# Two directions of a chunked scan: issued one after the other, or in step with each direction in its half of the array

## The chip, the cores and the metric

One core of one Trainium2 chip runs the whole program. The metric is the device time of one execution in microseconds (us); the time of a kernel is the median over its runs. Engines are named as in the profile: PE (TensorE matmul), PEld (TensorE weight load), DVE (VectorE), ACT (ScalarE), POOL (GpSimd), SP (SyncE, which issues the transfers).

## The reference, cut to what matters

The program is a hybrid attention block (two layers) followed by a second block: a gated delta-rule scan over 256 context rows, then the same scan over the 256 latent rows, starting from the state that the context left; then an output projection and a mixture of 16 experts. The scan runs in two directions, forwards and on the flipped sequence, and the two outputs are added. Each direction has 4 heads of width 128 and goes through 4 chunks of 64 rows:

```python
def step(state, xs):
    q_i, k_i, u_i, w_i, a_i, gl_i = xs
    v_new = u_i - w_i @ state
    o_i = q_i @ state + a_i @ v_new
    state = state * jnp.exp(gl_i)[..., None, None] + jnp.swapaxes(k_i, -1, -2) @ v_new
    return state, o_i
...
o_f, s_f = gdn_chunked(q, k, v, g[:, :, 0], beta[:, :, 0], s0_f)
o_b, s_b = gdn_chunked(flip(q), flip(k), flip(v), flip(g[:, :, 1]), flip(beta[:, :, 1]), s0_b)
return o_f + flip(o_b), s_f, s_b
```

The context scan needs only its final states; the latent scan needs the outputs, and not its last state.

## The kernel before, in words

The 256 rows lie in two tiles of 128 partitions (`tt`); each tile holds two chunks of 64 rows, one in partitions 0 to 63 and one in 64 to 127 (`HALF`). Direction `d` = 0 goes through the chunks 0, 1, 2, 3 and `d` = 1 through 3, 2, 1, 0. So at step `st` the one direction is always in one half of the partitions and the other direction in the other half.

`gdn_uw` (L1388) makes, for each of the four pairs (`tt`, `d`), `u` and `w` of both chunks of the tile. It transposes `v` (L1264), scales it with beta into `vb` (DVE, L1396) and `k` into `kb` (POOL, L1398), multiplies `G` with `vb` in `chunk_dots` (L1316; the two halves of the partitions in turn, all into one PSUM bank), copies the result to `U[tt, d]` (ACT, L1401), multiplies `kb` with `G` (L1406, the two halves in turn into two banks) and copies that to `WT[tt, d]` (ACT, L1409).

`gdn_scan` (L1424) is a generator. For each step it does direction 0 and then direction 1, and yields after each: `W` times state (L1444: all 128 rows of the array, 64 of its columns, 4 products), the sum into 64 partitions of `U` (DVE, L1445), the decay of the state (POOL, L1448), for the latent rows `Q` times state into the output bank (L1451: again 128 rows and 64 columns), `kg` times `U` (L1457: 64 rows and 128 columns) and the new state (ACT L1460 in the first context step, else DVE L1462). `kg` itself is made once for each pair (POOL, L1440; two buffers). After every second step the latent scan adds `aT` times `U` for both halves (L1467). An fp32 product stands in the trace as two matmul records, so 4 products are x8.

Around it: `block2` zips the context scan with `tinv_64` of the latent rows (a chain of 16 links of a `chunk_dots` and a DVE sum, L1537 to L1547), and the latent scan with `parts`, which are `chunk_mlp` (projections at L433 to L435 and L457, a gelu, norms and a product at L1595) and `scan_gate` (two more projections). The source only sets priorities: a list planner of the tile framework orders each engine's queue when the program is built, which is why projections that stand later in the source (L433 to L435 for `v` and `q`) lie in PE's queue between the products of the scan.

PSUM: `bank()` hands out five banks; the latent scan holds two of them for its outputs. SBUF: the pools of block 2 lie one behind the other in the order of `B2`, where `kg` stands in the middle. The expert weights are fetched ahead of time into a ring of 21 buffers (`ring`, 1 MB each) that lie over the same memory, and into the 2 buffers `w` of the projections; each fetch waits on SP's queue until what lay there is used up. The fetches of the projections (`load2`, L1179) and of the output projection (`rows_out`, L466) go through the same queue.

Of the kernel before, what the change touches and what calls it, by code (L numbers as in the profile page):

```python
# [32 lines left out]
HALF = slice(0, 64), slice(64, 128)  # L33
XB = 4
# [213 lines left out]
class Kern:  # L248
# [1125 lines left out]
    def gdn_attn(self, R):  # L1374
# [3 lines left out]
        for tt in range(2):  # L1378
# [5 lines left out]
            for d in range(2):  # L1384
                R["aT", tt, d] = aT[:, 8 * d + 4 * tt:8 * d + 4 * tt + 4, :]
                self.nc.vector.tensor_mul(R["aT", tt, d], self.decay(R, tt, d), kq)

    def gdn_uw(self, R):  # L1388

        nc = self.nc  # L1390
        G = R["G"]
        for tt in range(2):
            pv = self.nat(R, "v", tt)
            for d in range(2):
                vb = self.blk("vb", 2)
                nc.vector.tensor_mul(vb, pv, self.per_row(R["beta"][:, tt, 4 * d:4 * d + 4]))  # L1396
                kb = self.blk("kb", 2)
                nc.gpsimd.tensor_mul(kb, R["hat", "k", tt], self.per_row(R["be"][:, tt, d, :]))  # L1398
                pu = self.chunk_dots(G[tt, d], vb)
                R["U", tt, d] = self.blk("Ub" if tt ^ d else "Ua", 2)  # L1400
                nc.scalar.copy(R["U", tt, d], pu)  # L1401

                pw = [self.bank()[:, :, :64] for _ in HALF]
                for h in range(4):
                    for b, p in zip(HALF, pw):
                        nc.tensor.matmul(p[:, h, :], kb[b, h, :], G[tt, d][b, h, :], start=True, stop=True)  # L1406
                R["WT", tt, d] = self.blk("Wb" if tt ^ d else "Wa", 2)
                for b, p in zip(HALF, pw):
                    nc.scalar.copy(R["WT", tt, d][:, :, b], p)  # L1409

# [13 lines left out]
    def gdn_scan(self, R, S=None):  # L1424


        nc = self.nc
        o = None
        if S is not None:
            R["o"] = o = [self.bank() for _ in range(2)]  # L1430
        kg, touched = {}, set()
        S = S or [None, None]
        for st in range(4):
            for d in range(2):
                tt, hf = divmod(st if d == 0 else 3 - st, 2)
                rows = slice(64 * hf, 64 * hf + 64)
                U = R["U", tt, d]
                if (tt, d) not in kg and not (o and st == 3):
                    kg[tt, d] = self.blk("kg", 2)
                    nc.gpsimd.tensor_mul(kg[tt, d], R["hat", "k", tt], self.per_row(R["eg"][:, 1, tt, d, :]))  # L1440
                if S[d] is not None:
                    p = self.bank()
                    for h in range(4):
                        nc.tensor.matmul(p[rows, h, :], R["WT", tt, d][:, h, rows], S[d][:, h, :], start=True, stop=True)  # L1444
                    nc.vector.tensor_add(U[rows], U[rows], p[rows])  # L1445
                    if not (o and st == 3):
                        Se = self.blk("X", XB)
                        nc.gpsimd.tensor_mul(Se, S[d], self.per_row(R["egl"][:, 2 * tt + hf, 4 * d:4 * d + 4]))  # L1448
                if o:
                    for h in range(4):  # L1450
                        nc.tensor.matmul(o[tt][rows, h, :], R["Q", tt, d][:, h, rows], S[d][:, h, :],  # L1451
                                         start=(h == 0 and (tt, hf) not in touched), stop=False, skip_group_check=True)
                    touched.add((tt, hf))
                if not (o and st == 3):
                    p = self.bank()
                    for h in range(4):
                        nc.tensor.matmul(p[:, h, :], kg[tt, d][rows, h, :], U[rows, h, :], start=True, stop=True)  # L1457
                    n = self.blk("S", 4)
                    if S[d] is None:
                        nc.scalar.copy(n, p)  # L1460
                    else:
                        nc.vector.tensor_add(n, Se, p)  # L1462
                    S[d] = n
                if o and st % 2:
                    for h in range(4):
                        for b in HALF:
                            nc.tensor.matmul(o[tt][b, h, :], R["aT", tt, d][b, h, :], U[b, h, :], start=False, stop=False,  # L1467
                                             skip_group_check=True)
                yield
        R["S"] = S  # L1470

    def tinv_16(self, A, C, O, L, M, T):
# [474 lines left out]
```

## Time and profile before

| | |
|---|---|
| time, median of 3 runs | 1303.93 us (1303.8 to 1306.29) |
| the profiled execution's own time | 1295.95 us |
| its span in the profile | 1294.2 us |
| busy, share of the span | PE 81%, PEld 57%, DVE 43%, ACT 30%, POOL 20% |
| mean granted TensorE clock | 0.893 |
| HBM read and written | 328.6 MB, 254 GB/s over the span |

The rows below come from the one profiled execution. Its own time is the span plus the 1.75 us that lie around it; it is 8 us under the median of the runs, so a sum made from the rows is a difference, which is then taken off the median.

### The profile page before, as it was taken

Reading aid. Unit: us, or ns where it says so; the run is one execution under the profiler, and the core shown is the slowest. Engines: PE = TensorE matmul, PEld = TensorE weight load, DVE = VectorE, ACT = ScalarE, POOL = GpSimd, SP = SyncE. Lnnn points to the kernel's source line nnn. Section 1 sums busy time; section 2 is a strip of 40 time slices with the busy share of each in tenths; the row PEclk is TensorE's granted clock in tenths of the full one; section 3 lists DMA queues with packets and bytes.
Section 4 is the critical chain, followed back from the end, with each engine's and each line's share of the span. In section 5 each row is a group of like instructions: output and inputs, shape, how many; then the busy total and the mean of one; then the engine's idle time right before and its main releaser. Section 6 shows DMA issues by size and latency. Waiting matters only on the chain.

```text
span 1294.2 us, 22853 instructions
## 1 busy us (share of the span) xinstructions
PE 1048.7 (81%) x9488; PEld 733.4 (57%) x9488; DVE 558.6 (43%) x1315; ACT 387.4 (30%) x899; POOL 264.6 (20%) x235
## 2 busy tenths in 40 slices
PE   5878999986869999957879999898666766676665
PEld 2766787776757876736778888654322432232232
DVE  2585357777696445586585435620100010010002
ACT  2334337635334425525542434310000000000002
POOL 1431132266421221152424343200000000000000
PEclk9899999999989999977979999899877787787777
DMA  8745864434224385521211555979999999999996
GB/s 357 263 160 204 311 228 171 140 130 176 102 88 168 140 305 191 215 78 39 95 58 40 192 202 215 363 288 417 421 420 419 421 419 420 419 420 420 420 421 247
DMA packets 52569, 330.07 MB, mean 255 GB/s; under 512 B 8049, under 2 KB 9969, under 8 KB 14321
## 3 DMA queue, kind: packets, MB, share of 16 engines
q1 hardware_dynamic: 52464, 328.61, 64.9%
q8 instruction: 74, 1.21, 0.4%
q14 instruction: 31, 0.25, 0.1%
HBM read 327.54 MB, written 1.05 MB: 254 GB/s over the span
## 4 chain that ended last, share of the span: by engine, by line
PE 42%; DMA 35%; DVE 11%; POOL 4%; ACT 4%; issue 4%; POOLq 0%; SPq 0%; DVEq 0%; ACTq 0%
DMA rw<-in_w_up 13%; DMA rw<-in_w_down 11%; DMA rw<-in_w_gate 5%; PE mm L433 4%; PE mm L435 4%; PE mm L434 4%; DMA w<-in_w_up 3%; PE s L476 3%; PE mm L457 3%; PE g L372 3%; DMA wg<-in_w_ada 3%; POOL wl L345 2%; PE s L1316 2%; ACT wh L344 2%; PE s L553 2%
## 5 line engine op out<-in xcount | busy, mean ns | idle before, releaser
L433 PE MATMUL mm<-uT,wh 128*128 128x256 f32 x576 | 173.1, 301 | 11.1 <-DVE yT L1247 6.6
L435 PE MATMUL mm<-uT,wl 128*128 128x256 f32 x576 | 167.7, 294 | 15.9 <-DVE wl L345 9.2
L344 ACT CAST wh<-w 128x1024 fp32r<-128x1024 f32 x124 | 127.6, 1033 | 154.1 <-PE mm L434 114.9
L434 PE MATMUL mm<-uT,wh 128*128 128x256 f32 x576 | 167.4, 291 | 0.0
L345 POOL TENSOR_TENSOR wl<-w,wh 128x1024 fp32r<-128x1024 f32 x47 | 114.2, 2431 | 200.3 <-ACT wh L344 168.1
L435 PEld LDWEIGHTS mm<-uT,wl 128*128 128x128 f32 x576 | 111.6, 195 | 25.9 <-DVE wl L345 10.1
L433 PEld LDWEIGHTS mm<-uT,wh 128*128 128x128 f32 x576 | 112.6, 196 | 22.7 <-issue 14.5
L1808 PE MATMUL g<-rw,XE 128*32 128x256 f32 x928 | 84.2, 469 | 41.3 <-DMA rw<-in_w_up 41.3
L345 DVE TENSOR_TENSOR wl<-w,wh 128x1024 fp32r<-128x1024 f32 x77 | 96.6, 1254 | 43.9 <-ACT wh L344 43.5
L434 PEld LDWEIGHTS mm<-uT,wh 128*128 128x128 f32 x576 | 112.4, 195 | 5.2 <-issue 4.0
L1808 PE MATMUL o<-rw,XE 128*32 128x256 f32 x944 | 85.3, 464 | 32.8 <-DMA rw<-in_w_gate 32.8
L1824 DVE TENSOR_TENSOR hd<-hd,g 128x256 f32<-128x256 f32 x16 | 6.7, 419 | 214.4 <-PE g L1808 214.4
L1820 ACT ACTIVATE hd<-o 128x256 f32<-128x256 f32 x16 | 6.1, 384 | 310.9 <-PE o L1808 310.9
L1852 PE MATMUL mm<-rw,hT 128*32 128x256 f32 x880 | 67.9, 446 | 18.7 <-DMA rw<-in_w_down 13.2
L1808 PEld LDWEIGHTS g<-rw,XE 128*32 128x32 f32 x928 | 31.8, 128 | 86.1 <-DMA rw<-in_w_up 66.8
L1808 PEld LDWEIGHTS o<-rw,XE 128*32 128x32 f32 x944 | 31.1, 125 | 76.8 <-DMA rw<-in_w_gate 53.9
L457 PE MATMUL mm<-wh,uT 128*128 128x256 f32 x256 | 54.0, 298 | 3.1 <-ACT wh L344 2.5
L1852 PEld LDWEIGHTS mm<-rw,hT 128*32 128x32 f32 x880 | 27.9, 124 | 49.5 <-DMA rw<-in_w_down 21.7
L457 PEld LDWEIGHTS mm<-wh,uT 128*128 128x128 f32 x256 | 41.6, 194 | 7.1 <-ACT wh L344 2.9
L565 ACT ACTIVATE P<-s,nm 128x256 f32<-128x256 f32 (+1 forms) x88 | 35.8, 419 | 18.9 <-DVE nm L558 18.7
L476 PE MATMUL s<-wh,m 128*128 128x512 f32 x128 | 41.2, 401 | 0.0
L457 PE MATMUL mm<-wl,uT 128*128 128x256 f32 x128 | 37.9, 296 | 0.8 <-DVE wl L345 0.7
(644 smaller groups left out, 1987.9 us busy)
## 6 DMA issues: line engine op xcount, KB each, us to landing
rw<-in_w_gate SPq DMA_DIRECT2D x59, 1024.0 KB, 19.9
rw<-in_w_up SPq DMA_DIRECT2D x58, 1024.0 KB, 19.9
rw<-in_w_down SPq DMA_DIRECT2D x55, 1024.0 KB, 19.8
w<-in_w_in SPq DMA_DIRECT2D x48, 1024.0 KB, 4.7
wg<-in_w_mod SPq DMA_DIRECT2D x24, 1024.0 KB, 4.9
wg<-in_w_ada SPq DMA_DIRECT2D x21, 1024.0 KB, 5.3
w<-in_w_out SPq DMA_DIRECT2D x12, 1024.0 KB, 4.8
w<-in_w_up SPq DMA_DIRECT2D x6, 1024.0 KB, 19.8
```

Source lines behind the costliest of these rows:

```text
L344: self.nc.scalar.copy(hi, w)
L345: self.lo_engine().tensor_sub(lo, w, hi)
L372: nc.tensor.matmul(p[32 * j:32 * j + 32, :], vec[:, 2 * q + kk, :], w[:, kk, 256 * j:256 * j + 256], start=(kk == 0 and (q == 0 or not who ...
L433: mm(out, wh[:, k, :], uh[:, k, :], start=(k == 0), stop=False)
L434: mm(out, wh[:, k, :], ul[:, k, :], start=False, stop=False)
L435: mm(out, wl[:, k, :], uh[:, k, :], start=False, stop=(k == 7))
L457: mm(p[:, tt, :], a[:, k, t], b[:, k % 4, :], start=(k == 0 and tt == 0 and j == 0), stop=(k == 7 and j == 2), skip_group_check=True)
L476: mm(Y(tt, n), a[:, t], b[:, 512 * n:512 * n + 512], start=(k2 == 0 and kk == 0 and i == 0), stop=(k2 == 3 and kk == 1 and i == 2))
L553: nc.tensor.matmul(S[:, h, o:o + n], qT[rows, t], kT[rows, :n], start=False, stop=True, skip_group_check=True)
L565: nc.scalar.activation(Pm[:, h, o:o + n], S[:, h, o:o + n], AF.Exp, bias=nm[:, i:i + 1], scale=0.125, accum_out=l[:, i:i + 1])
L1808: nc.tensor.matmul(pp[32 * j:32 * j + 32, :], XE[:, k, 32 * (e % 4):32 * (e % 4) + 32], w[:, kk, 256 * j:256 * j + 256], start=(k == 0), s ...
L1852: nc.tensor.matmul(py[32 * j:32 * j + 32, :], hT[:, cb, 32 * jj:32 * jj + 32], w[:, kk, 256 * j:256 * j + 256], start=(k == 0), stop=(k == 7))
```

## The change

`gdn_scan` does a step for both directions at once. For each head it issues the product of direction 0 and then that of direction 1, whose operands or results lie in the other half of the partitions; `W` times state of both directions goes into one bank, and one DVE sum of 128 partitions takes it into `U`. `kg` times `U` goes into two banks. `Q` times state now comes after `kg` times `U`, and `aT` times `U` follows in every step. The scan yields twice after each step. For this `U` is laid out by steps: `U[st]` holds the chunk of direction 0 in its half and that of direction 1 in the other. `gdn_uw` therefore transposes both tiles of `v` at the start, goes through the pairs as (0, 0), (1, 1) and then (1, 0), (0, 1), and for each two makes two `u` products and then two `w` products. `kg` gets four buffers in place of two.

```diff
--- before.py
+++ after.py
@@ -1385,26 +1385,39 @@
                 R["aT", tt, d] = aT[:, 8 * d + 4 * tt:8 * d + 4 * tt + 4, :]
                 self.nc.vector.tensor_mul(R["aT", tt, d], self.decay(R, tt, d), kq)
 
+    @staticmethod
+    def step_of(st):
+
+
+        return [(c // 2, HALF[c % 2]) for c in (st, 3 - st)]
+
     def gdn_uw(self, R):
 
         nc = self.nc
         G = R["G"]
-        for tt in range(2):
-            pv = self.nat(R, "v", tt)
-            for d in range(2):
-                vb = self.blk("vb", 2)
-                nc.vector.tensor_mul(vb, pv, self.per_row(R["beta"][:, tt, 4 * d:4 * d + 4]))
-                kb = self.blk("kb", 2)
-                nc.gpsimd.tensor_mul(kb, R["hat", "k", tt], self.per_row(R["be"][:, tt, d, :]))
-                pu = self.chunk_dots(G[tt, d], vb)
-                R["U", tt, d] = self.blk("Ub" if tt ^ d else "Ua", 2)
-                nc.scalar.copy(R["U", tt, d], pu)
+        pv = [self.nat(R, "v", tt) for tt in range(2)]
+        for s2 in range(0, 4, 2):
+            vb, kb = {}, {}
+            pairs = [(s2 // 2, 0), (1 - s2 // 2, 1)]
+            for tt, d in pairs:
+                vb[tt, d] = self.blk("vb", 2)
+                nc.vector.tensor_mul(vb[tt, d], pv[tt], self.per_row(R["beta"][:, tt, 4 * d:4 * d + 4]))
+                kb[tt, d] = self.blk("kb", 2)
+                nc.gpsimd.tensor_mul(kb[tt, d], R["hat", "k", tt], self.per_row(R["be"][:, tt, d, :]))
+            for st in (s2, s2 + 1):
+                pu = self.bank()
+                for h in range(4):
+                    for d, (tt, b) in enumerate(self.step_of(st)):
+                        nc.tensor.matmul(pu[b, h, :], G[tt, d][b, h, :], vb[tt, d][b, h, :], start=True, stop=True)
+                R["U", st] = self.blk("Ub" if s2 else "Ua", 2)
+                nc.scalar.copy(R["U", st], pu)
+            for tt, d in pairs:
 
                 pw = [self.bank()[:, :, :64] for _ in HALF]
                 for h in range(4):
                     for b, p in zip(HALF, pw):
-                        nc.tensor.matmul(p[:, h, :], kb[b, h, :], G[tt, d][b, h, :], start=True, stop=True)
-                R["WT", tt, d] = self.blk("Wb" if tt ^ d else "Wa", 2)
+                        nc.tensor.matmul(p[:, h, :], kb[tt, d][b, h, :], G[tt, d][b, h, :], start=True, stop=True)
+                R["WT", tt, d] = self.blk("Wb" if s2 else "Wa", 2)
                 for b, p in zip(HALF, pw):
                     nc.scalar.copy(R["WT", tt, d][:, :, b], p)
 
@@ -1431,42 +1444,50 @@
         kg, touched = {}, set()
         S = S or [None, None]
         for st in range(4):
-            for d in range(2):
-                tt, hf = divmod(st if d == 0 else 3 - st, 2)
-                rows = slice(64 * hf, 64 * hf + 64)
-                U = R["U", tt, d]
-                if (tt, d) not in kg and not (o and st == 3):
-                    kg[tt, d] = self.blk("kg", 2)
+            at = list(enumerate(self.step_of(st)))
+            more = not (o and st == 3)
+            U = R["U", st]
+            for d, (tt, b) in at:
+                if (tt, d) not in kg and more:
+                    kg[tt, d] = self.blk("kg", 4)
                     nc.gpsimd.tensor_mul(kg[tt, d], R["hat", "k", tt], self.per_row(R["eg"][:, 1, tt, d, :]))
-                if S[d] is not None:
-                    p = self.bank()
-                    for h in range(4):
-                        nc.tensor.matmul(p[rows, h, :], R["WT", tt, d][:, h, rows], S[d][:, h, :], start=True, stop=True)
-                    nc.vector.tensor_add(U[rows], U[rows], p[rows])
-                    if not (o and st == 3):
-                        Se = self.blk("X", XB)
-                        nc.gpsimd.tensor_mul(Se, S[d], self.per_row(R["egl"][:, 2 * tt + hf, 4 * d:4 * d + 4]))
-                if o:
-                    for h in range(4):
-                        nc.tensor.matmul(o[tt][rows, h, :], R["Q", tt, d][:, h, rows], S[d][:, h, :],
-                                         start=(h == 0 and (tt, hf) not in touched), stop=False, skip_group_check=True)
-                    touched.add((tt, hf))
-                if not (o and st == 3):
-                    p = self.bank()
-                    for h in range(4):
-                        nc.tensor.matmul(p[:, h, :], kg[tt, d][rows, h, :], U[rows, h, :], start=True, stop=True)
-                    n = self.blk("S", 4)
+            Se = [None, None]
+            if S[0] is not None:
+                p = self.bank()
+                for h in range(4):
+                    for d, (tt, b) in at:
+                        nc.tensor.matmul(p[b, h, :], R["WT", tt, d][:, h, b], S[d][:, h, :], start=True, stop=True)
+                nc.vector.tensor_add(U, U, p)
+                if more:
+                    for d, (tt, b) in at:
+                        Se[d] = self.blk("X", XB)
+                        e = 2 * tt + (b.start > 0)
+                        nc.gpsimd.tensor_mul(Se[d], S[d], self.per_row(R["egl"][:, e, 4 * d:4 * d + 4]))
+            if more:
+                p = [self.bank() for _ in range(2)]
+                for h in range(4):
+                    for d, (tt, b) in at:
+                        nc.tensor.matmul(p[d][:, h, :], kg[tt, d][b, h, :], U[b, h, :], start=True, stop=True)
+                N = [self.blk("S", 4) for _ in range(2)]
+                for d in range(2):
                     if S[d] is None:
-                        nc.scalar.copy(n, p)
+                        nc.scalar.copy(N[d], p[d])
                     else:
-                        nc.vector.tensor_add(n, Se, p)
-                    S[d] = n
-                if o and st % 2:
-                    for h in range(4):
-                        for b in HALF:
-                            nc.tensor.matmul(o[tt][b, h, :], R["aT", tt, d][b, h, :], U[b, h, :], start=False, stop=False,
-                                             skip_group_check=True)
-                yield
+                        nc.vector.tensor_add(N[d], Se[d], p[d])
+            if o:
+                for h in range(4):
+                    for d, (tt, b) in at:
+                        nc.tensor.matmul(o[tt][b, h, :], R["Q", tt, d][:, h, b], S[d][:, h, :],
+                                         start=(h == 0 and (tt, b.start) not in touched), stop=False, skip_group_check=True)
+                touched.update((tt, b.start) for d, (tt, b) in at)
+                for h in range(4):
+                    for d, (tt, b) in at:
+                        nc.tensor.matmul(o[tt][b, h, :], R["aT", tt, d][b, h, :], U[b, h, :], start=False, stop=False,
+                                         skip_group_check=True)
+            if more:
+                S = N
+            yield
+            yield
         R["S"] = S
 
     def tinv_16(self, A, C, O, L, M, T):
```

## Rows read from the trace of the kernel before

**Rows 1.** Windows: stretch, length, busy us by engine (instructions), granted clock, DMA share, GB/s.

```profile
676.00:727.00 51.00, 49.74 (x609) 43.56 (x608) 25.29 (x46) 17.55 (x31) 19.78 (x17) 0.98 0.22 74
727.00:748.00 21.00, 17.40 (x153) 14.68 (x151) 10.48 (x16) 10.04 (x30) 8.15 (x8) 0.92 0.69 250
748.00:802.00 54.00, 53.10 (x441) 47.98 (x442) 25.20 (x37) 21.14 (x33) 20.78 (x19) 1.00 0.51 181
802.00:830.00 28.00, 25.47 (x121) 19.48 (x120) 18.99 (x31) 13.17 (x34) 7.74 (x4) 1.00 0.89 348
830.00:852.00 22.00, 17.97 (x106) 14.42 (x109) 10.55 (x41) 3.49 (x10) 0.00 (x0) 0.77 0.63 263
```

**Rows 2.** PE's waits from 676 to 802: us in total, times, longest.

```profile
PE s L1457 <- DVE Ub L1445: 1.3, 1, 1.3
```

**Rows 3.** Critical chain, 796 to 880: start, us until the next piece, what.

```profile
855.76 12.88 DMA rw<-in_w_up
```

**Rows 4.** Windows of 640 to 830 for L1444, for L1457 and for L1451 alone: PE, PEld.

```profile
640.00:830.00 190.00, 15.22 (x112) 11.85 (x112) 0.95 0.45 163
...
640.00:830.00 190.00, 16.93 (x112) 13.98 (x112) 0.95 0.45 163
...
640.00:830.00 190.00, 8.72 (x64) 7.15 (x64) 0.95 0.45 163
```

**Rows 5.** Critical chain, 640 to 830: start, us until the next piece, what.

```profile
684.91 1.02 PE s L1444 x8
...
687.07 1.08 PE s L1457 x8
...
749.92 0.87 PE s L1451 x8
```

**Rows 6.** Timeline, PE, 714 to 728: start, length, line, form; halves of the partitions in turn.

```profile
717.47 1.09 PE L1316 MATMUL s<-vb,E 64*64 64x128 f32 x16
718.49 1.11 PE L1406 MATMUL s<-E,kb 64*128 64x64 f32 x16
719.53 0.66 PE L1264 MATMUL s<-c,yT 128*128 128x128 f32 x4
```

**Rows 7.** Timeline, PE, 107.4 to 112: products in column strips, in row halves, in the whole array.

```profile
107.52 1.07 PE L372 MATMUL g<-wg,cv 128*32 128x256 f32 x16
...
108.83 0.92 PE L553 MATMUL s<-qk 64*128 64x256 f32 x8
109.69 1.13 PE L400 MATMUL g<-gacc,c 128*128 128x256 f32 x4
```

**Rows 8.** Timeline, one step of one direction in the context scan.

```profile
684.84 1.09 PE L1444 MATMUL s<-S,Wa 128*64 128x128 f32 x8
...
685.96 0.68 DVE L1445 TENSOR_TENSOR Ua<-Ua,s 64x512 f32<-64x512 f32 x1 [0.54 <-PE s L1444]
...
687.00 1.16 PE L1457 MATMUL s<-Ua,kg 64*128 64x128 f32 x8
...
688.26 0.69 DVE L1462 TENSOR_TENSOR S<-X,s 128x512 f32<-128x512 f32 x1 [1.62 <-PE s L1457]
```

**Rows 9.** Instructions of L1448 and of L1401: count, shortest, median and longest in ns.

```profile
L1448 POOL TENSOR_TENSOR X<-S,legl x6: 1040/1041/1245, 708.0 to 774.7; 128x512 f32<-128x512 f32 x6
...
L1401 ACT COPY Ua<-s x4: 586/586/586, 649.8 to 724.3; 128x512 f32<-128x512 f32 x4
```

**Rows 10.** Waits of SP's queue over the span: us in total, times, longest.

```profile
SPq L1846 <- PE s L1457: 14.2, 1, 14.2
```

**Rows 11.** Timeline, SP, 700 to 900: issues of the output projection's weights.

```profile
790.62 0.33 SPq L466 DMA_DIRECT2D w<-in_w_out  x1
...
799.78 0.33 SPq L466 DMA_DIRECT2D w<-in_w_out  x1
```

**Rows 12.** The page, transfers: count, KB each, median us from issue to landing.

```profile
rw<-in_w_gate SPq DMA_DIRECT2D x59, 1024.0 KB, 19.9
...
w<-in_w_out SPq DMA_DIRECT2D x12, 1024.0 KB, 4.8
```

## The prediction, made before the result was known

> **What bounds the kernel now.** I read the windows by stage first. From 676 to 727 (the context scan beside a chain of the latent inverse) PE is busy 49.74 of 51 us, and from 748 to 802 (the latent scan beside the projections) 53.10 of 54; apart from its own weight loads no other engine is over half busy in either [rows 1]. In between, from 727 to 748, PE has only 17.40 of 21 us: there a chain through ACT, DVE and POOL sets the pace. The waits say the same: the longest that PE has in the scans on a sum of theirs is 1.3 us [rows 2]. So both scans are bound by the work in PE's queue, not by the latency of a step: the planner has put projections into the holes. A faster step therefore gains only as far as PE time is removed, and then it gains nearly all of that.
>
> What comes after decides whether the gain lasts. In 830 to 852 the transfers rest (DMA share 0.63) [rows 1]: the weight buffers are full before the first expert product frees one. Then PE waits 12.88 us for a weight in one piece [rows 3], and the rest is bound by transfers. Their second run begins when the first buffer comes free, so time taken off before 852 should move the whole tail forward, as long as the prefetch is still complete. From 727 to 852 the DMA engines rest 21 × 0.31 + 54 × 0.49 + 28 × 0.11 + 22 × 0.37 = 44 us [rows 1], more than the change can take away.
>
> **The change part by part.** *Products of the scan.* L1444 has 112 records, L1457 112, L1451 64 [rows 4], that is 14, 14 and 8 groups of 8 records. A group holds PE for 1.02, 1.08 and 0.87 us until the next piece [rows 5]: 14.3 + 15.1 + 7.0 = 36.4 us. In the changed kernel the same records stand in 7, 7 and 4 groups of 16, in which neighbours lie in different halves of the array.
>
> What does a group of 16 cost? The nearest row is L1316: 16 records with 128 moving columns, the two diagonal quarters in turn, start at 717.47 and the next piece at 718.49: 1.02 us, as long as 8 records of L1444 alone [rows 6]. So two halves that differ in rows and in columns run beside each other. The new pairs differ in one of them only.
>
> For `W` and `Q` (all rows, half of the columns) the bounds are 16 records at 1.02 (full overlap) and at 2.04 (none). L372 has this form with four column strips: 16 records with 256 columns in 1.07 us, where 4 records over the whole array take 1.13, tails included [rows 7]. Strips with the same rows overlap. I take 1.02.
>
> For `kg` (half of the rows, all columns) the bounds are 1.04 and 2.16. L1406 has this form with half as many moving columns and takes 1.04 us for 16 [rows 6]; by itself that fits serial work too. L553 speaks for overlap: 4 records of 256 and 4 of 128 columns (the row names the first form), row halves in turn, are done in 0.92, while 4 of 256 over the whole array alone take 1.13 [rows 7]. I take 1.04.
>
> The sum after is 7 × 1.02 + 7 × 1.04 + 4 × 1.02 = 18.5 us, so 36.4 - 18.5 = 17.9 us leave PE: in the context scan 3 × 1.02 + 4 × (2.16 - 1.04) = 7.5, in the latent scan 4 × 1.02 + 3 × 1.12 + 4 × (1.74 - 1.02) = 10.4.
>
> One rule speaks against the larger half of it. The Trainium skill, "TensorE: Matmul & The Clock Gate", section "Part 3: Packing small matmuls", says that a weight load overlaps products in flight only where the row groups differ. The column halves of `W` and `Q` share all rows; by that rule they would run in turn. L372's strips share them as well and overlap [rows 7], so this trace disagrees with it for strips of 32 columns; for halves of 64 no run here shows it yet.
>
> *Latency of a step.* Before, `kg` starts 687.00 - 684.84 = 2.16 us after `W`, and the state's sum begins 1.26 us after `kg` and takes 0.69: 4.1 us for one direction [rows 8], and the two directions alternate, 8.2 for both. After, both need about 1.02 + 1.14 + 1.04 + 0.2 + 2 × 0.69 = 4.8. The holes (1.14 between `W` and `kg`, about 1.6 between `kg` and the next `W`) go from two pairs of them a step to one, so fewer projections are wanted to fill them; in the latent scan `Q` and `aT`, 2.0 us, now stand in the second. I cost the holes at nothing because the same projections cover them; uncovered they would be 7 × 2.7 = 19 us.
>
> *DVE, POOL, ACT.* The sum into `U` costs 0.68 us for 64 partitions and the state's sum 0.69 for 128 [rows 8]: width is free, so 14 sums become 7, 4.8 us less DVE, off the bound. POOL's decays (1.04) and ACT's copies (0.59) [rows 9] keep their count. The first decay and sum of a step are ready before the second, which is why the next `W` waits for two sums; that is in the 4.8.
>
> *`gdn_uw`.* The same 16 + 16 records for each pair and the same copies. But two transposes of `v` now hold two of the five banks to the end, and three are left for one `u` and two `w`: the second `w` can wait for an ACT copy of 0.59 [rows 9]. Bounds: nothing, and 0.6 for each half, 2.4 us in both calls. In the latent call projections stand behind it; I take nothing.
>
> *`kg` with four buffers.* It removes POOL's waits for the old ones. It also moves what lies behind it in memory by half a weight buffer, so some weight fetches wait for other lines than before; no fetch is added. I take nothing; its price is the rival below.
>
> *What is passed on.* The latent scan runs where PE is 98% busy: I take 9 tenths of 10.4, 9.4. The context scan's gain must pass the stretch that is not bound by PE, where 17.40 of 21 us are PE's; whole it would be 7.5, and a third if that chain begins no earlier than before. I take two thirds, 5.0. Together 14.4 us. The profiled execution of 1295.95 would become 1281.6. The median of the runs lies 8 us above it, which I keep: 1303.9 - 14.4 = 1289.5.
>
> **The rivals.** *Column halves run in turn* (the skill's rule above). `W` and `Q` then save nothing: 7.1 + 2.9 of the 17.9 go, and of the other 7.8 the same share is passed on, 14.4 / 17.9 = 0.8, so 6.3 are left: 1297.6. Against it is L372. Chance 0.08.
>
> *Row halves run in turn* when the weights have all 128 columns. `kg` saves nothing: 10.0 × 0.8 = 8.0 are left: 1295.9. For it is the lone L1406 row, against it L553. Chance 0.08. Were both true, the change would do nothing of what it says, and the time would stay within the bound of "same".
>
> *The gain is not passed on.* The projections that fill PE hang on a cast, a split and two buffers `w`; if they come no sooner, PE only idles where it now works. Then the context part is lost and a quarter of the latent part remains: 2.6 us, 1301.3. For it: the 727 to 748 stretch. Against it: 98% busy in the stretches beside it. Chance 0.14, half of it on each side of 0.2%.
>
> *Slower: a fetch of the output projection gets stuck behind a weight fetch.* SP's queue already waited 14.2 us for the last reads of `kg` [rows 10], and the output projection's fetches stand in the same queue, 9.2 us apart [rows 11]. With the memory moved and more weight fetches ready at once, one of them could wait those 14.2 us and then land like a weight fetch, 19.9 us, in place of 4.8 [rows 12]: 14.2 + 15.1 - 9.2 (its partner buffer still feeds PE) = 20 us late, and the stretch from 802 to 830, where PE is busy 25.47 of 28 [rows 1], stands still for it: 1303.9 - 14.4 + 20 = 1309.5. It decides once the delay is above 14.4 us. Against it: the same queue has this order already and PE has no such wait. Chance 0.10.
>
> **How the numbers follow.** The likeliest is full overlap, 1289.5, with chance 0.60; its own range is 1285 (all 17.9, and a little of the idle time before 676) to 1295 (half). The range for all is 1283 to 1302: it takes in both part overlaps and the rival without passing on, and leaves out the slower one and the ends. Within 0.2% (2.6 us, about what a measurement of this kernel can tell from no change) I count half of the "not passed on": 0.07. Slower is 0.10. Faster is 0.60 + 0.08 + 0.08 + 0.07 = 0.83.
>
> **What the profile after would show.** Groups of 16 records of the new products with about 1.0 us until the next piece; 2.0 in one of the forms would name that rival. One step of both directions in about 5 us. One sum into `U` for each step, of 128 partitions and 0.69 us. The stretch from the context scan to the end of the latent one shorter by 12 to 18 us, PE still over 95% busy in the scans, and the first expert weight freed near 838 with the DMA engines at rest just before. If instead PE's busy share in the scans falls below 90%, the gain was not passed on. Wrong altogether I would be if the planner orders the projections so that the holes of a step stay open, or if the granted clock (0.98 to 1.00 in the scans [rows 1]) falls with the sparser stream.

## The result and the profile after

The changed kernel takes 1286.99 us (median of 4 runs, 1286.40 to 1289.38), the kernel before 1303.87 us beside it (4 runs, 1302.89 to 1306.29): a ratio of 0.9871, 95% interval 0.9853 to 0.9890. Forecast were 1289.5 us and 1283 to 1302. The profiled execution took 1286.54 us, its span is 1284.8 us.

The windows of the kernel after, in the stretches of [rows 1]:

```profile
676.00:727.00 51.00, 49.22 (x642) 44.18 (x643) 27.54 (x47) 19.80 (x47) 22.09 (x19) 0.94 0.31 111
727.00:748.00 21.00, 17.25 (x167) 13.62 (x167) 9.77 (x16) 8.31 (x16) 8.34 (x8) 0.92 0.74 291
748.00:802.00 54.00, 46.13 (x429) 40.29 (x424) 28.55 (x50) 24.22 (x48) 20.71 (x17) 1.00 0.53 198
802.00:830.00 28.00, 24.25 (x118) 19.57 (x117) 15.31 (x30) 9.81 (x20) 5.32 (x3) 0.86 0.96 389
830.00:852.00 22.00, 20.56 (x219) 13.93 (x221) 8.25 (x29) 3.87 (x7) 0.00 (x0) 0.95 0.54 219
```

In the context scan PE is still busy 49.22 of 51 us. In the latent scan it is busy 46.13 of 54, where it was 53.10: the first sign that part of the gain was lost there. (The latent scan now ends at 791.4. In its own stretch, C to D below, PE is busy 41.89 of 47.5 us, 88%, where it was 51.45 of 52.1.)

The critical chain of the kernel after, with the pieces that answer to [rows 5] and the first weight of the tail [rows 3]:

```profile
687.35 1.02 PE s L1459 x16
...
695.58 1.16 PE s L1470 x16
...
747.53 1.02 PE s L1480 x16
...
853.03 16.29 DMA rw<-in_w_up
```

Sixteen records now take 1.02 (`W`, L1459), 1.09 to 1.16 (`kg`, L1470) and 1.02 us (`Q`, L1480), as long as eight did. (The first `W` group, at 680.86, takes 1.65 us; the granted clock of 678 to 684 is 0.66.) The step of both directions, timeline of after, from one `W` group to the next [rows 8]:

```profile
687.28 1.09 PE L1459 MATMUL s<-S,Wb 128*64 128x128 f32 x16
688.42 0.69 DVE L1460 TENSOR_TENSOR Ub<-Ub,s 128x512 f32<-128x512 f32 x1 [0.54 <-PE s L1459]
689.45 1.16 PE L1470 MATMUL s<-Ub,kg 64*128 64x128 f32 x16
691.42 1.28 DVE L1476 TENSOR_TENSOR S<-X,s 128x512 f32<-128x512 f32 x2
693.70 1.09 PE L1459 MATMUL s<-S,Wb 128*64 128x128 f32 x16
```

It takes 6.4 us, not 4.8: VectorE comes to the state's sums only at 691.42, because a split of a weight (L345, 690.28, 1.23 us) is in its queue ahead of them.

PE's longest waits after, 744 to 800 (us in total, times, longest):

```profile
PE mm L1616 <- POOL uv L1613: 2.5, 1, 2.5
PE mm L435 <- POOL wl L345: 1.2, 2, 0.8
PE s L1470 <- DVE Ua L1460: 1.0, 1, 1.0
PE mm L1697 <- DVE e L1694: 1.0, 1, 1.0
PE s L1470 <- DVE Ub L1460: 0.8, 1, 0.8
```

All but that of L1697 lie in the latent scan: 5.5 us, where the kernel before had 0.6, on a sum into `U` (L1457).

**Where the time went.** Five marks cut the span of each profiled execution: A, the last latent projection product (L1340); B, the last sum of the latents' inverse (L1568, before L1547); C, the last transposes of `Q` (L1433, before L1420); D, the last `aT` product (L1485, before L1467); E, the first expert product (L1829, before L1808). Each is the first or last start of its line's rows, weight loads included. B and C hold the context scan's gain, D the latent scan's. The medians and ratios (each to the runs of before taken beside it, 95% interval) stand with them:

| kernel | median us | ratio to before | A | A-B | B-C | C-D | D-E | E-end |
|---|---|---|---|---|---|---|---|---|
| before | 1303.87 | | 643.8 | 70.3 | 34.4 | 52.1 | 47.7 | 445.9 |
| e0 before again | 1301.76 | 1.0012 [0.9984, 1.0040] | 646.0 | 73.3 | 34.6 | 52.1 | 48.9 | 445.6 |
| after | 1286.99 | 0.9871 [0.9853, 0.9890] | 646.6 | 62.9 | 34.4 | 47.5 | 47.7 | 445.7 |
| e4 after again | 1287.34 | 0.9914 [0.9888, 0.9941] | 646.6 | 62.9 | 34.4 | 47.4 | 47.8 | 445.6 |
| e1 not in turn | 1291.15 | 0.9921 [0.9887, 0.9954] | 650.0 | 64.7 | 34.5 | 48.9 | 47.7 | 445.4 |
| e2 `kg` not in turn | 1297.01 | 0.9969 [0.9940, 0.9998] | 646.1 | 63.1 | 35.8 | 53.3 | 50.7 | 445.4 |
| e3 `W`, `Q` not in turn | 1291.42 | 0.9937 [0.9906, 0.9968] | 644.0 | 64.1 | 34.4 | 50.0 | 50.7 | 445.5 |
| e10 layout alone | 1305.48 | 1.0018 [0.9988, 1.0047] | 649.8 | 75.0 | 33.9 | 54.1 | 46.5 | 445.6 |
| e7 `W` thrice, latent | 1293.15 | 0.9959 [0.9933, 0.9986] | 648.0 | 63.0 | 34.4 | 55.5 | 46.5 | 445.6 |
| e8 `W` thrice, context | 1295.55 | 0.9971 [0.9947, 0.9996] | 647.3 | 68.1 | 33.6 | 48.6 | 49.2 | 445.5 |
| e5 z casts first | 1286.90 | 0.9915 [0.9880, 0.9950] | 644.2 | 63.0 | 34.4 | 47.1 | 47.7 | 445.6 |
| e6 MLP on VectorE | 1292.04 | 0.9929 [0.9905, 0.9953] | 646.3 | 63.0 | 34.3 | 48.1 | 50.7 | 445.6 |
| e9 z0 before ws | 1285.10 | 0.9885 [0.9848, 0.9921] | 644.8 | 63.0 | 34.4 | 47.3 | 47.8 | 445.6 |
| e11 both | 1289.26 | 0.9905 [0.9870, 0.9939] | 649.7 | 63.0 | 34.3 | 46.4 | 49.1 | 445.6 |

The tail from E on is the same within 0.5 us in every kernel, so a gain ahead of E is passed on whole.

From A to E the two executions of before take 204.5 and 208.9 us, mean 206.7; the two of after 192.5. Against the mean 14.2 us are gone: 9.0 from A to C, 4.65 from C to D, the rest behind D. But the two executions of before differ by the granted clock. These windows are A-B of before, of e0 and of after:

```profile
643.80:714.10 70.30, 60.05 (x654) 52.77 (x651) 49.53 (x104) 22.23 (x36) 26.34 (x23) 0.88 0.17 57
646.00:719.30 73.30, 63.07 (x652) 55.21 (x647) 49.60 (x104) 22.12 (x36) 26.23 (x23) 0.84 0.18 55
646.60:709.50 62.90, 53.76 (x658) 47.13 (x653) 48.20 (x100) 23.75 (x39) 28.16 (x24) 0.89 0.17 57
```

D-E goes the same way: 47.7 us at 0.89 in before and in after, 48.9 at 0.86 in e0. The first execution of before has about the clock of after in all four stretches (0.88, 0.95, 1.00, 0.89 and 0.89, 0.95, 1.00, 0.89), so this pair is the fair one: 12.0 us from A to E, 7.4 of them from A to C, 4.6 from C to D, none behind D. PE's busy time from A to E falls from 183.17 to 166.53 us, 16.6 less. The medians show more (16.9 us, or 12.8 for e4 and the runs beside it). The clock may be a part of that: the three executions with one direction after the other (before, e0, e10) have 0.88, 0.84 and 0.84 in A-B, the eleven with both in step 0.86 to 0.90. Whether the change raises the clock there was not tested.

### The profile page after: what moved, and what is told of

It is laid out like the page before. It is cut to its first block, busy times and chain, and to the rows that moved or that the text cites. A ratio compares the mean times of both kernels' runs of the same rounds, so it can differ in the third digit from the quotient of the medians.

```text
span 1284.8 us, 22839 instructions
## 1 busy us (share of the span) xinstructions
PE 1036.9 (81%) x9488; PEld 724.4 (56%) x9488; DVE 554.6 (43%) x1308; ACT 386.9 (30%) x899; POOL 264.4 (21%) x235
## 4 chain that ended last, share of the span: by engine, by line
PE 40%; DMA 35%; DVE 11%; POOL 5%; ACT 4%; issue 4%; SPq 0%; POOLq 0%; DVEq 0%; ACTq 0%
DMA rw<-in_w_up 15%; DMA rw<-in_w_down 11%; DMA rw<-in_w_gate 5%; PE mm L433 4%; PE mm L435 4%; PE mm L434 4%; PE s L476 3%; POOL wl L345 3%; DMA wg<-in_w_ada 3%; PE g L372 3%; PE mm L457 3%; PE s L1316 2%; ACT wh L344 2%; PE o L582 2%; PE s L553 2%
## 5 line engine op out<-in xcount | busy, mean ns | idle before, releaser
L345 POOL TENSOR_TENSOR wl<-w,wh 128x1024 fp32r<-128x1024 f32 x47 | 114.4, 2437 | 201.7 <-ACT wh L344 166.0
L345 DVE TENSOR_TENSOR wl<-w,wh 128x1024 fp32r<-128x1024 f32 x77 | 98.2, 1275 | 52.1 <-ACT wh L344 49.3
L1829 PE MATMUL g<-rw,XE 128*32 128x256 f32 x928 | 84.6, 471 | 39.4 <-DMA rw<-in_w_up 39.4
L1829 PE MATMUL o<-rw,XE 128*32 128x256 f32 x944 | 88.3, 479 | 32.0 <-DMA rw<-in_w_gate 32.0
L1873 PE MATMUL mm<-rw,hT 128*32 128x256 f32 x880 | 63.7, 424 | 22.9 <-DMA rw<-in_w_down 17.5
L1829 PEld LDWEIGHTS g<-rw,XE 128*32 128x32 f32 x928 | 32.0, 128 | 85.3 <-DMA rw<-in_w_up 65.9
L1829 PEld LDWEIGHTS o<-rw,XE 128*32 128x32 f32 x944 | 31.7, 129 | 77.8 <-DMA rw<-in_w_gate 52.9
```

The source lines that it names most:

```text
L345: self.lo_engine().tensor_sub(lo, w, hi)
L1829: nc.tensor.matmul(pp[32 * j:32 * j + 32, :], XE[:, k, 32 * (e % 4):32 * (e % 4) + 32], w[:, kk, 256 * j:256 * j + 256], start=(k == 0), s ...
L1873: nc.tensor.matmul(py[32 * j:32 * j + 32, :], hT[:, cb, 32 * jj:32 * jj + 32], w[:, kk, 256 * j:256 * j + 256], start=(k == 0), stop=(k == 7))
```

## The experiments

**e0, before again**, for the spread.

> The kernel before, unchanged. The two traces so far differ by 9.4 us of span, the medians by 16.9 us: the one profiled execution of before (1295.95 us) lies 7 to 8 us under all its other runs. Theory A: that execution was an exception, and a new profiled execution of before shows a span of about 1302 us, with the extra 7 to 8 us in one place (a stretch bound by transfers, or the granted clock). Rival B: the profiled executions of before are always near 1296 and its unprofiled ones near 1304; then this one shows 1294 to 1297 again, and the medians differ by something that no trace shows.

1301.76 us, no difference, but single runs reach from 1296.76 to 1309.26, and its profiled execution is 6.3 us longer in span than the one of the prediction: theory A, though not in one place. 2.2 us of it lie ahead of A, 3.0 in A-B and 1.2 in D-E, the last two at a lower granted clock. A alone, ahead of which nothing was edited in any kernel, lies between 643.8 and 650.0 in the table. Stretches between marks are the better measure, where their clocks agree.

**e1 to e3, products not in turn.** The step of both directions stays; the loops over heads and directions change places, in all three products (e1), for `kg` alone (e2), for `W` and `Q` (e3):

```
-                for h in range(4):
-                    for d, (tt, b) in at:
+                for d, (tt, b) in at:
+                    for h in range(4):
```

> The changed kernel, but each of its three scan products is issued for direction 0 with all four heads and then for direction 1; layout, steps, sums and buffers stay. Theory A (the halves of the array overlap, and that is what the change gains): a group of 16 takes about 2.0 us until the next piece in place of 1.0, 17.9 us come back to PE; the context part of it (7.5) is passed on whole and of the latent part (10.4) about half, so the time rises by 9 to 16 us over the changed kernel's 1287.0: 1296 to 1303. Rival B (the gain is the shorter step, with fewer sums and holes, and the projections hide the products anyway): 1287 plus or minus 3.

> The changed kernel with only kg times U not in turn (the row halves). Theory A: 4 groups in the context scan and 3 in the latent one go from about 1.1 to about 2.1 us; 4.5 us passed on whole and 3.4 about half: plus 4 to 8 us, 1291 to 1295. Rival B (row halves with 128 weight columns gain little): under 2 us, 1286 to 1289.

> The changed kernel with only W times state and Q times state not in turn (the column halves). Theory A: 3 groups of W in the context scan (3.1 us, passed on whole), 4 of W and 4 of Q in the latent one (7.0 us, about half): plus 4 to 10 us, 1291 to 1297. Rival B (the rule that halves with the same rows run in turn): under 2 us, 1286 to 1289.

e1 takes 1291.15 us, between the two theories and nearer to B: the gain that the forecast put on the turn stayed for the most part. The critical chain of e1 shows why:

```profile
691.41 1.51 PE s L1459 x16
694.07 1.64 PE s L1470 x16
...
753.90 1.51 PE s L1480 x16
```

Not in turn, 16 records take 1.51 to 1.64 us, neither 1.02 nor 2.04: the second direction's eight begin beside the first one's last records. From A to E e1 takes 195.8 us, 3.3 more than after. So the turn itself is worth about 3 us here (4 by the medians; by the ratios, each to its own runs of before, 1 to 6.5).

e2 (1297.01 us, above both of its ranges) and e3 (1291.42, in that of theory A) undo less than e1 but took longer in C-D and D-E. Windows of e2 and of e3 show a granted clock of 0.66 and 0.58 there, so for a part of the time the lower of its two levels (1.2 of 2.4 GHz), with PE at work nearly throughout in the first:

```profile
770.00:780.00 10.00, 9.95 (x65) 8.66 (x66) 3.92 (x10) 0.42 (x2) 3.71 (x4) 0.66 0.60 235
```

```profile
820.00:836.00 16.00, 13.37 (x58) 11.38 (x58) 9.32 (x32) 3.58 (x11) 0.00 (x0) 0.58 0.95 390
```

After had 1.00 and 0.68 there. Their times give no share for `kg` and none for `W` and `Q`; they are inconclusive. Only in A-B, where the granted clock is 0.89 in after and in all three, can they be compared: e2 is 0.2 us longer there than after, e3 1.2 and e1 1.8 (one execution each).

**e10, the layout alone.** `u` by steps and its product stay, the scan goes one direction after the other as before:

```
-            at = list(enumerate(self.step_of(st)))
...
+            for d, (tt, b) in enumerate(self.step_of(st)):
...
-                for h in range(4):
-                    for d, (tt, b) in at:
+                if S[d] is not None:
+                    p = self.bank()
+                    for h in range(4):
                         nc.tensor.matmul(p[b, h, :], R["WT", tt, d][:, h, b], S[d][:, h, :], start=True, stop=True)
-                nc.vector.tensor_add(U, U, p)
+                    nc.vector.tensor_add(U[b], U[b], p[b])
```

> The changed kernel's layout of u by steps, its product of u and its four kg buffers stay, but the scan goes as before: one direction's step after the other's, eight products at a time, each direction's sums on its own 64 rows. Theory A, the forecast's (all that counts is that 16 products of both halves stand next to each other): no gain is left but that of the aT products, 1298 to 1303 us, and groups of 8 at 1.02 us again. Theory E (a part of the gain comes with the layout: one product of u for both directions, the earlier kg): 1290 to 1297 us.

1305.48 us, ratio 1.0018: no gain, theory A, and a little above its range. Its groups, critical chain:

```profile
692.39 1.09 PE s L1470 x8
...
694.08 1.02 PE s L1456 x8
```

With e1 this splits the change: the layout gives nothing, both directions in one step 13.7 us from A to E (209.5 to 195.8, one execution each), the turn another 3.3. The medians give 14.3 and 4. The 13.7 is an upper figure, since e10 had a granted clock of 0.84 in A-B and e1 0.89. Against the first execution of before, with 0.88 there, e1 gains 8.7 us (204.5 to 195.8). What of this comes from neighbouring products, from the joint sum or from the single chain of steps was not separated.

**e4, after again.**

> The changed kernel once more, for its spread and for stretches to compare with. Theory A, the forecast's own: its time lies 0.9 to 1.5% under that of the kernel before, and the tensor engine is over 95% busy in the last scan. Theory B, from the trace of after: the same time, but the stretch from the last latent projection product to the last sum of the latents' inverse (62.7 us after, 70.0 before) has gained 7 to 10 us and the stretch from the last Q transposes to the last aT product (47.5 after, 52.1 before) only 4 to 5, in every execution, because in the latter the tensor engine waits for the gelu chain of the MLP.

1287.34 us, and theory B: 62.9 and 47.4 us, the first execution's stretches over again.

**e7 and e8, products added.** `W`'s products three times over, in the latent scan (e7) or in the context scan (e8, `not o`); each time they start afresh, so the result is the same:

```
-                for h in range(4):
+                for _ in range(3 if o else 1):
+                  for h in range(4):
                     for d, (tt, b) in at:
                         nc.tensor.matmul(p[b, h, :], R["WT", tt, d][:, h, b], S[d][:, h, :], start=True, stop=True)
```

> The changed kernel with the W x S products of the last (latent) scan issued three times over, each time afresh, so that the result stays: 2 x 16 products more in each of its four steps, 4 x 2 x 1.09 = 8.7 us of the tensor engine, on the path of the steps as well. Theory A, the forecast's (this scan is bound by the tensor engine, nine tenths pass on): the stretch from the last Q transposes to the last aT product grows by 7.8 to 8.7 us. Theory B (the first three steps are done early, while the tensor engine waits for the MLP chain): the first steps' 6.5 us fall into its waits, and only the last step's 2.2 us and some 1 to 2 us more are seen: 2 to 4 us.

> The changed kernel with the W x S products of the first (context) scan issued three times over, each time afresh, so that the result stays: 2 x 16 products more in each of the three steps that have them, 3 x 2 x 1.09 = 6.5 us of the tensor engine. Theory A, the forecast's (two thirds of what the tensor engine is given there pass on): the stretch from the last latent projection product to the last sum of the latents' inverse grows by 4.4 us. Theory B (this stretch is bound by the tensor engine through and through, or by the chain of the steps, which is made longer by the same sum): it grows by 6 to 7 us. Theory C (the inverse's own chain holds the stretch): under 3 us.

e8: 6.5 us of products make A-B 5.2 us longer, at about the same granted clock (0.90, after 0.89). That is eight tenths, between theories A and B. From A to E it is 7.0, but 2.6 of these lie in C-D and D-E, where nothing was edited and the clock was lower (0.96 and 0.86; after 1.00 and 0.89).

e7: C-D grows by 8.1 of 8.7 us. That is the number of theory A, and against mine. But PE wasn't bound by its work alone there either: from C to D it idles for 5.6 us, as it does in after. The longest waits, 742 to 802:

```profile
PE s L1460 <- DVE S L1477: 2.5, 1, 2.5
PE mm L1617 <- POOL uv L1614: 2.4, 1, 2.4
```

Three windows of e7, cut at the last `u` product, with which the MLP's chain begins, and at the ws product (L1617), show where the 8.1 us are:

```profile
745.40:762.10 16.70, 16.29 (x180) 15.12 (x177) 4.33 (x5) 4.21 (x5) 4.47 (x3) 1.00 0.32 105
762.10:775.48 13.38, 8.55 (x135) 7.67 (x133) 7.61 (x13) 6.42 (x7) 5.77 (x6) 1.00 0.75 276
775.48:800.90 25.42, 25.02 (x252) 23.30 (x254) 11.68 (x15) 9.31 (x14) 7.86 (x8) 0.93 0.39 139
```

After takes 14.9, 12.9 and 19.7 us for these. Ahead of the chain e7 takes 1.8 us more: the first step's added products. Beside the chain it takes 0.5 more, with PE as busy as in after (8.59 us): the second step's added products and a part of the third's stand there, but the third step waits 2.5 us for the state's sum, and the rest of it, with `kg` and `aT`, comes behind the ws product. There it takes 5.7 more: that rest, the last step's products, and the lower clock, whose part can't be told apart. So the waits beside the chain took up nothing: PE's queue is in order, and what is added in one place moves other work behind the ws product.

**e5, e6, e9, e11, the MLP's chain.** Four attempts to take the waits of the latent scan away. e5 sends the casts of the MLP's result behind the last z cast that was issued when they are made:

```
+        def lhs_halves(k):
+            with self.after(mlp["cast"]):
+                return self.act_halves(lhs[k], "X", XB)
```

> The four casts of the MLP's result for w_out2, which stand in ScalarE's queue ahead of the casts of the z weights and waited 8.3 us for GpSimd, are sent behind two of these (or all four); nothing else moves. Theory B (the last scan is held by the MLP chain, through this queue): the z projection begins some 6 to 8 us earlier, the last step of the scan with it, the stretch from the last Q transposes to the last aT product falls from 47.5 to 41 to 45 us, and the kernel gains 3 to 6 us on the changed one (0.2 to 0.45%). Theory A (the last scan is bound by the tensor engine's products alone): no change, within 1 us. Theory C (the scan's own chain of steps holds it): no change either, but the z projection is then done early and the last step still ends at the same time.

C-D 47.1 us: theory B fell for this queue. The z cast, timeline of ScalarE in e5, now waits as long for PE to free a buffer of the z weights:

```profile
775.37 1.05 ACT L344 CAST wh<-w 128x1024 fp32r<-128x1024 f32 x1 [9.25 <-PE mm L434]
```

e6 moves GpSimd's three products to VectorE (one of the three lines is shown), e9 sends the first half of z ahead in program order, e11 does both:

```
-                nc.gpsimd.tensor_mul(yy, yy, s[:, 2 * a:2 * a + 2, :])
+                nc.vector.tensor_mul(yy, yy, s[:, 2 * a:2 * a + 2, :])
...
-        parts = chain(self.chunk_mlp(uT, mlp), self.scan_gate(uT, mlp))
+        cm, sg = self.chunk_mlp(uT, mlp), self.scan_gate(uT, mlp)
+        parts = chain(islice(cm, 4), islice(sg, 1), cm, sg)
```

> The changed kernel with GpSimd's three products of the latent MLP (the squares, the gain, and the product with u) on VectorE. Theory B (with shorter scan products, the chain gelu - squares - norm - gain - ws product - z projection, in the order of TensorE's queue, holds the last scan; TensorE waits 2.5 us in it): the chain to the ws product gets shorter by about half of GpSimd's 2.05 and 2.88 us (VectorE takes 0.70 us for such a block), so the stretch from the last Q transposes to the last aT product falls from 47.4 to 45 to 46 us and the kernel by 1.5 to 2.5 us. Theory A (the scan is bound by the tensor engine's products): no change, within 0.5 us. Theory D (VectorE is late with the scan's own sums then): 0 to 2 us longer.

> The changed kernel with the first half of the z projection sent ahead of the last part of the MLP (its norm's scaling, ws product and product with u), so that TensorE's queue has 48 products (5.8 us), whose weights are there, ahead of the ws product for which it waits 2.5 us. Theory B (the MLP's chain in TensorE's queue holds the last scan): the wait for the gain is filled, the buffers of the z weights come free earlier, the stretch from the last Q transposes to the last aT product falls from 47.4 to 42.5 to 45 us and the kernel by 2.5 to 5 us. Theory A (bound by the products alone): no change, within 0.5 us. Theory C (the steps' own chain holds it): the wait for the gain goes, another of the same size comes in at the last step; no change.

> Both edits at once: the first half of the z projection ahead of the MLP's last part, and GpSimd's three products of the MLP on VectorE. Theory B: the two take from the same wait, so that together they give little more than the larger alone: the stretch from the last Q transposes to the last aT product at 42 to 44.5 us (47.4 in the changed kernel), the kernel 3 to 5.5 us faster than the changed one and about 17 to 20 us faster than before. Theory A: no change from the changed kernel, within 0.5 us.

C-D 48.1, 47.3 and 46.4 us: none gave what was expected, and no version is measurably faster than the changed one. PE's longest wait in each, 742 to 802 (e6, e9, e11):

```profile
PE s L1459 <- DVE S L1476: 2.4, 1, 2.4
```

```profile
PE mm L1616 <- POOL uv L1613: 4.3, 1, 4.3
```

```profile
PE mm L1616 <- ACT aff L657: 3.3, 1, 3.3
```

In e6 VectorE is late with the state's sum (theory D). In e9 the z products do fill a part, but the third step's `W` now stands behind the first half of the ws product, whose wait grew to 4.3 us. The timeline shows what made the chain longer in e9: GpSimd has a split of the z weights in its queue, and VectorE's first scaling of `gv` (L1612), which starts in that split, takes 2.74 us, where it takes 0.69 in after. In e11 the same happens to a sum of the norm (L416), which takes 0.17 us in after. VectorE and GpSimd of e9, then of e11:

```profile
767.05 2.40 POOL L345 TENSOR_TENSOR wl<-w,wh 128x1024 fp32r<-128x1024 f32 x1 [0.46 <-ACT wh L344]
767.26 2.74 DVE L1612 TENSOR_TENSOR uv<-uv,gvrs 128x512 f32<-128x512 f32 x1
...
772.09 2.40 POOL L345 TENSOR_TENSOR wl<-w,wh 128x1024 fp32r<-128x1024 f32 x1
772.19 2.33 DVE L416 TENSOR_TENSOR gvqb<-gvqb,gvqa 128x8 f32<-128x8 f32 x1
```

So each of these two chains lost about 2.1 us beside such a split. The trace puts the ws product's wait in e11 on the sigmoid of z; the gain product (L1613, 776.76, 0.68 us) had ended 0.1 us before the ws product began at 777.55, and which of the two held it was not tried. The granted clock takes part as well: it was 0.96 from C to D in e6, e9 and e11 and 1.00 in after, and PE was busy 43.89, 42.58 and 42.69 us there for as many records as after has in 41.89.

What these four have in common is the time of the MLP's chain on PE's queue, from the `W` group that follows the last `u` product to the ws product (L1616): 12.7 us in after and in e5, 13.7, 14.5 and 15.4 in e6, e9 and e11. The windows from the last `u` product to the ws product, before and then after:

```profile
764.90:779.10 14.20, 13.61 (x123) 11.63 (x121) 9.05 (x17) 6.43 (x7) 7.79 (x8) 1.00 0.64 224
```

```profile
758.80:771.70 12.90, 8.59 (x125) 7.31 (x123) 8.92 (x16) 6.42 (x7) 5.73 (x6) 1.00 0.80 303
```

Before, the scan's products filled the chain's 14.2 us (13.61 busy). After, 5.0 us less of them leave 12.9: only 1.3 us came out, and PE idles for 4.3 of them (0.6 before). No edit here made the chain itself shorter, so that it holds C-D is read from these windows and not shown: whether C-D would follow a shorter chain stays open.

## Why the prediction was right

The total was near, and the mechanism of the products was right; two shares in its sum were not, and their errors cancel in part. That the total is as near as it is, is luck.

- **Groups of 16 as long as 8: right, shown.** 1.02, 1.09 to 1.16 and 1.02 us. Both "in turn" rivals are out. The Trainium skill's rule ("TensorE: Matmul & The Clock Gate", "Part 3: Packing small matmuls") that a weight load overlaps products in flight only where the row groups differ, from which the prediction made the first of these rivals, disagrees with `W` and `Q` here: 16 records in 1.02 us, for halves of 64 too.
- **17.9 us leave PE because of the turn: 16.6 us left it, but the turn is the smaller part of the cause.** e1 shows that neighbours not in turn already overlap in part: 16 at about 1.5. By its group times e1 leaves 7 × (2.04 - 1.51) + 7 × (2.16 - 1.64) + 4 × (1.74 - 1.51) = 8.3 us; PE's busy time from A to E falls by 10.7 (183.17 to 172.47). At a like clock 8.7 us of time went. The other 9.6 us of product time bought 3.3.
- **"A faster step gains only as far as PE time is removed": no run speaks against it, but "nearly all of that" was too much.** Against the execution of before with a like clock e1 gains 8.7 us and after 12.0, for 10.7 and 16.6 us less of PE. (Against the mean of both executions of before, e1 would have gained 10.9, but that counts the lower clock of e0.)
- **Context part, two thirds of 7.5 = 5.0: too low.** 7.4 us from A to C at a like clock, and e8's added 6.5 were passed on with 5.2. As an estimate, the 0.01 between the clocks of before and after is worth under 1 us (3.0 us for 0.04 between before and e0), so the share is eight to nine tenths. The stretch B-C, at which the prediction feared a loss, is 34.4 us in both kernels. Why so much passes is argued, not shown: the inverse's products stand in PE's queue behind the scan's, so B and all that hangs on it moves by what PE saves.
- **Latent part, 9 tenths of 10.4 = 9.4: too high.** 4.65 us, at a granted clock of 1.00 in all four executions. The prediction's step "runs where PE is 98% busy: I take 9 tenths" failed: 98% said that PE was full before, not that the MLP's chain had slack beside it. That chain took 14.2 us and had 0.6 us of it uncovered; by the windows it became the bound as soon as 5 us of cover went. PE's waits in the latent scan grew from 0.6 to 5.5 us; these 4.9 (3.7 of them beside the chain) and the 4.65 make 9.6 of the 10.4. The prediction said that PE would stay over 95% busy in the scans, and that under 90% the gain was not passed on: it was 97% in the context scan and 88% from C to D.
- **Sum.** 7.4 + 4.6 = 12.0 at a like clock, the lower end of the 12 to 18 that the prediction gave for the two scans, forecast 14.4; against the mean of both executions of before 9.0 + 4.65 + 0.55 behind D = 14.2. By the medians it is 16.9 us, and 12.8 for e4 (1300.18 beside it): executions of one kernel spread that far, and the 8 us between profile and median that the forecast kept are of that spread (e0).
- **Step latency 4.8 us: 6.4.** VectorE's queue, not PE, ends it. In the context scan, where it was read, it cost nothing that the runs show: PE is busy 49.22 of 51 us there.
- **Tail: right.** First expert product at 839.1 ("near 838"), E to the end unchanged. The fetch that gets stuck on SP, the slower rival, did not come: D-E is 47.7 us in both, and PE's longest wait in the output projection is 1.3 us, for a split. `gdn_uw` and the four `kg` buffers at nothing: e10 has both and is within 0.5% of before, but a small cost isn't excluded, since its A-B and C-D are 1.7 and 2.0 us longer than e0's at the same granted clock (0.84 and 1.00).

## What to carry to other kernels

A full engine hides the chains beside it. Before costing a cut at nine tenths, take the time of each chain that the engine's work covers, from its first to its last instruction, and subtract: what the cut leaves under the longest chain is, by the reading of the latent scan, not passed on. And waits in an in-order queue are no room for more work: in e7 PE waited 4.8 us beside the chain, and yet the products added to its queue made the scan 8.1 us longer. How far this holds without the lower clock of e7, and for a scan whose chain is shorter, was not tried.

Doing both directions in one step, so that products of both halves of the array stand next to each other, came before issuing them in turn: here the first gave some 9 to 14 us, the second some 3 to 4.

Before two executions are compared by stretches, compare their granted clocks by stretches as well: here two executions of one kernel differ by 4.4 us between A and E, and both stretches that differ by more than 0.2 us have different clocks.

## What the runs showed of the hardware beside this

- Eight records on one half of the array and then eight on the other, not in turn, take 1.51 to 1.64 us, between 1.02 (in turn) and 2.04 (apart): a part of them overlaps by itself.
- The granted clock differs between executions behind the scans, where nothing was edited, and the time of D-E goes with it: 46.5 us at 0.93 (e7, e10), 47.7 or 47.8 at 0.89 (before, after, e1, e4, e5, e9), 48.9 to 49.2 at 0.86 (e0, e8, e11), 50.7 at 0.83 (e2, e3, e6).
- A VectorE instruction that started in a 2.40 us split on GpSimd (L345) lasted until the split was over or a little longer: 2.74 us for 0.69 in e9 (L1612), 2.33 for 0.17 in e11 (L416), and 2.14 for 0.17 in after (L415, at 728.33). Not every one does: L1558 took its usual 0.41 us beside the split at 704.33 in after.
